# An order of weight sums and splits ahead of and in a squared-ReLU MLP

## The chip, the cores and the metric

The kernel is one program on one core of a Trainium2 chip. The metric is the device time of one execution in microseconds (us). TensorE (PE) multiplies, VectorE (DVE) and ScalarE (ACT) do elementwise work, GpSimd (POOL) and SyncE (SP) here mostly issue transfers (DMAs); each engine runs its instructions in the order in which they stand.

## The reference

One layer of an encoder over 512 tokens of width 1024: a token mixer of recurrent heads, cross-attention over 256 memory tokens, and an MLP of hidden width 4096, with a residual each and a final RMSNorm. All in float32:

```python
for l in range(DEPTH):                       # DEPTH = 1
    x = x + token_mixer(rmsnorm(x, norm_mix[l]), w_in[l], b_in[l], ...)
    x = x + cross_attention(rmsnorm(x, norm_xattn[l]), rmsnorm(mem, norm_mem[l]), w_xq[l], w_xkv[l], w_xo[l])
    x = x + squared_relu_mlp(rmsnorm(x, norm_mlp[l]), w_up[l], w_down[l])
return rmsnorm(x, norm_final)

def squared_relu_mlp(xn, w_up, w_down):
    return jnp.square(jax.nn.relu(xn @ w_up)) @ w_down
```

## The kernel before, in words

**Products.** Every float32 operand is split into a high part (a copy rounded to the type that TensorE takes, by ScalarE) and a low part (the rest, by VectorE), both at L348 in `split_out`. A product is then three matmuls: high by high, high by low, low by high. For weights the tiles are `st` (a block of 128 x 1024 as loaded), `wh` and `wl` (its high and low part); each has three buffers. In the MLP `xT` and `yT` hold the parts of the input of the up product, `a` those of the hidden activations.

**Seven products for eight.** The MLP is four up stages and four down stages in turn (`st` 0 to 7, even ones up). Each is a blocked product done with seven products P1 to P7 in place of eight, in two halves g (written a and b: "7b" is half 1 of P7). P1 to P3 take a block of the weights as it is, P4 to P7 sums of blocks, and the inputs are sums likewise ("forms": `form(p, g, ...)`, built and split by VectorE and ScalarE). The list `MJ` gives the order in which the 14 halves of each stage are multiplied; in the first up stage it is 1a 1b 2a 2b 5a 5b 6a 6b 7a 7b 4a 3a 4b 3b, so its entry n = 9 is 7b. In down stages it is P1, P5, P6, P2, P7, P3, P4, each as a, b (P1, P5, P2, P6, P3, P7, P4 in the last).

**Sums of weights.** For the up stages, and in part for the down stages, they are made ahead of the MLP in HBM (`form_<stage>_<product>_<half>`): SyncE writes a first block (`start`) or copies another sum (`follow`, L321, a P4 sum from the P6 sum), GpSimd adds a block by an accumulating transfer (`add`, L305). `make_forms` gives the order of these steps, and `allow(n)` lets some of them go at each weight block: a budget to which n is added, of which a step of SyncE takes 1 and an add 2. `weights()`, called for each block of the stream ahead of the MLP, calls `allow`; so does `mahead()` inside the later products. A step of GpSimd is made to wait (`after`) for the last low split that was made, a step of SyncE stands behind (`behind`, an order on its engine without a wait) the last load of weights. GpSimd's adds stand in one row with its other work: the powers of the norms (L214, L1081, L1448) and accumulating loads of sums for the attention's output product (L1187).
The rest of the down stages' sums are made in two buffers in SBUF (`msum`, in the profile `as`): `sum_base` loads the first block by SyncE, `sum_add` adds by GpSimd. `due` says at which weight block they are issued: for P5 of the next down stage at n + 3 and n + 7.

**Order on the engines.** PE's order is written by hand; ACT and DVE are put in order by a scheduler after what is ready, with `behind` and `tc.high_priority()` as its marks. `msplit` splits weight block n and loads it if `mload` hasn't; `mahead(n)` splits up to n + 2 and loads up to n + 6. SyncE issues weight loads from L269 (the stream) and from L305 and L1239 (`mload`: blocks as they are, and the sums in HBM).

**Other lines.** L1490 builds P7's input of the first up stage from two others, L1493 that of P3; L1623 and L1628 take products of the first up stage out of the accumulators; L1556 and L1557 are ReLU and square (`square`), L1565 to L1583 subtractions and additions for the forms of a down stage, L1527 adds a product of a down stage to the residual (`add_to`), L1518 is the last scaling of a row tile, and L1519 its store. The dictionary `turn` gives after which product a form is built.

## Time and profile before

| | |
|---|---|
| three runs | 828.56, 827.82, 826.29 us (median 827.82) |
| profiled execution | 825.79 us, of which the span of the instructions 824.0 us |
| mean granted clock of TensorE | 0.998 |
| PE busy | 803.1 us (97%) |
| DVE, ACT, POOL busy | 618.6, 486.1, 95.4 us |
| weight splits at L348 (`wh`, `wl`) | 165 each, 1058 and 1224 ns |
| transfers | 167.26 MB, mean 203 GB/s |
| GpSimd's adds for sums in HBM | 44, 512 KB each, 9.0 us from issue to landing (median) |
| SyncE's copies between sums | 18, 512 KB each, 10.2 us to landing |
| SyncE's weight loads `st<-in_wpk` | 123, 512 KB each, 4.4 us to landing |

Times in rows are us from the start of the span; a row of a timeline gives start, length, engine, line, operation, out<-in, and in brackets for how long the engine stood idle ahead of it and who released it. `...` in a row of rows stands for rows left out.

### The profile page before, as it was taken

The page shows a single profiled execution, that of the slowest core. Times are in us where ns is not written, and L with a number is a line of the kernel's source. Part 1 is how long each engine was busy: PE and PEld are TensorE (multiplying, and loading weights), DVE is VectorE, ACT ScalarE, POOL GpSimd, SP SyncE. Part 2 cuts the span into 40 slices and gives each one's busy share as a digit, 9 for nine tenths or more (in the row PEclk, how much of TensorE's full clock was granted, in tenths as well). Part 3 has the DMA queues.
Part 4 walks back from the last instruction along what each step waited for, and adds up shares of the span by engine and source line. Part 5 has one row for each costly group of instructions (what it writes and reads, how often), then busy time and mean ns, then how long its engine had stood idle before and what let it go on. Part 6 is the DMA issues. An engine that isn't in the chain of part 4 may idle for free.

```text
span 824.0 us, 14080 instructions
## 1 busy us (share of the span) xinstructions
PE 803.1 (97%) x5438; PEld 693.2 (84%) x5438; DVE 618.6 (75%) x1033; ACT 486.1 (59%) x854; POOL 95.4 (12%) x130
## 2 busy tenths in 40 slices
PE   8999999999999999999999999899999999999995
PEld 6788788886888989887888889887998899789984
DVE  6568975699469988555567979897489658875995
ACT  5247464445578475455545678773586458546854
POOL 2000111220230011221111003010001000100001
PEclk9999999999999999999999999999999999999999
DMA  7368889588688676887884357768866696668552
GB/s 278 118 238 257 216 181 280 174 197 254 159 230 252 198 221 203 237 193 218 203 224 108 85 122 212 248 163 247 267 199 158 218 282 198 180 200 266 179 153 103
DMA packets 56597, 167.26 MB, mean 203 GB/s; under 512 B 5393, under 2 KB 5521, under 8 KB 56530
## 3 DMA queue, kind: packets, MB, share of 16 engines
q1 hardware_dynamic: 41200, 126.04, 43.7%
q0 software_dynamic: 15040, 39.85, 26.8%
q8 instruction: 43, 0.70, 0.3%
q10 hardware_dynamic: 290, 0.47, 0.2%
q14 instruction: 24, 0.20, 0.1%
HBM read 164.24 MB, written 48.23 MB: 258 GB/s over the span
## 4 chain that ended last, share of the span: by engine, by line
PE 72%; DVE 11%; DMA 6%; issue 5%; ACT 5%; POOL 1%; POOLq 0%; ACTq 0%; DVEq 0%
PE mm L351 11%; PE mm L352 11%; PE mm L353 11%; PE sm L1315 5%; PE sm L1316 4%; PE sm L1314 4%; DVE wl L348 4%; PE sm L1604 2%; DMA st<-in_wpk 2%; PE sm L1605 2%; PE sm L1603 2%; ACT wh L348 2%; DMA st<-form_P 2%; PE mm L1604 1%; PE mm L1605 1%
## 5 line engine op out<-in xcount | busy, mean ns | idle before, releaser
L348 DVE TENSOR_TENSOR wl<-st,wh 128x1024 fp32r<-128x1024 f32 x165 | 201.5, 1224 | 104.0 <-ACT wh L348 103.1
L348 ACT ACTIVATE wh<-st 128x1024 fp32r<-128x1024 f32 x165 | 174.2, 1058 | 171.2 <-PE mm L352 44.0
L351 PE MATMUL mm<-xT,wh 128*128 128x512 f32 x288 | 115.5, 402 | 0.0
L353 PE MATMUL mm<-xT,wl 128*128 128x512 f32 x288 | 113.1, 393 | 0.1
L352 PE MATMUL mm<-xT,wh 128*128 128x512 f32 x288 | 112.8, 392 | 0.3 <-DVE xT L1066 0.3
L305 POOL DMA_DIRECT2D form_P<-in_wpk x44 | 44.7, 1059 | 289.1 <-DVE wl L348 243.5
L1315 PE MATMUL sm<-wl,a 128*128 128x512 f32 x180 | 70.4, 391 | 1.8 <-DVE wl L348 1.8
L1314 PE MATMUL sm<-wh,a 128*128 128x512 f32 x180 | 70.3, 391 | 0.1
L1316 PE MATMUL sm<-wh,a 128*128 128x512 f32 x180 | 70.1, 390 | 0.0
L353 PEld LDWEIGHTS mm<-xT,wl 128*128 128x128 f32 x288 | 54.1, 188 | 11.8 <-DVE wl L348 0.3
L352 PEld LDWEIGHTS mm<-xT,wh 128*128 128x128 f32 x288 | 54.2, 188 | 10.9 <-DVE xT L1066 0.9
L351 PEld LDWEIGHTS mm<-xT,wh 128*128 128x128 f32 x288 | 54.1, 188 | 10.9 <-ACT wh L348 0.3
L305 POOL DMA_DIRECT2D as<-in_wpk x20 | 17.6, 915 | 262.0 <-DVE wl L348 159.8
L1315 PEld LDWEIGHTS sm<-wl,a 128*128 128x128 f32 x180 | 33.8, 188 | 10.0 <-DVE wl L348 3.0
L1314 PEld LDWEIGHTS sm<-wh,a 128*128 128x128 f32 x180 | 33.8, 188 | 7.6 <-ACT wh L348 0.5
L1316 PEld LDWEIGHTS sm<-wh,a 128*128 128x128 f32 x180 | 33.8, 188 | 6.9
L1603 PE MATMUL sm<-yT,wh 128*128 128x256 f32 x128 | 36.3, 284 | 1.7 <-ACT yT L348 1.7
L1604 PE MATMUL sm<-yT,wh 128*128 128x256 f32 x128 | 36.3, 284 | 0.9 <-DVE yT L348 0.9
L1604 PE MATMUL sm<-xT,wh 128*128 128x256 f32 x128 | 36.4, 284 | 0.3 <-DVE xT L348 0.2
L1604 PE MATMUL mm<-xT,wh 128*128 128x256 f32 x128 | 36.3, 284 | 0.2 <-DVE xT L348 0.2
L1603 PE MATMUL sm<-xT,wh 128*128 128x256 f32 x128 | 36.4, 284 | 0.0
L1603 PE MATMUL mm<-xT,wh 128*128 128x256 f32 x128 | 36.3, 284 | 0.0
(388 smaller groups left out, 2114.6 us busy)
## 6 DMA issues: line engine op xcount, KB each, us to landing
st<-in_wpk SPq DMA_DIRECT2D x123, 512.0 KB, 4.4
form_P<-in_wpk POOLq DMA_DIRECT2D x44, 512.0 KB, 9.0
st<-form_P SPq DMA_DIRECT2D x42, 512.0 KB, 5.8
form_P<-in_wpk SPq DMA_DIRECT2D x26, 512.0 KB, 8.0
as<-in_wpk POOLq DMA_DIRECT2D x24, 512.0 KB, 8.4
form_P<-form_P SPq DMA_DIRECT2D x18, 512.0 KB, 10.2
gate<-in_wpk POOLq DMA_DIRECT2D x8, 512.0 KB, 5.8
as<-form_P SPq DMA_DIRECT2D x8, 512.0 KB, 6.6
```

Source lines behind the costliest of these rows:

```text
L305: return eng.dma_start(out=dst, in_=mblock(st, g, *b), max_dma_last_dim=4096, **kw)
L348: return sc.activation(dst_hi, src, AF.Copy), v.tensor_tensor(out=dst_lo, in0=src, in1=dst_hi.bitcast(F32), op=ALU.subtract)
L351: pe.matmul(ps, lhsT=ah, rhs=bh, start=first, stop=False)
L352: pe.matmul(ps, lhsT=ah, rhs=bl, start=False, stop=False)
L353: pe.matmul(ps, lhsT=al, rhs=bh, start=False, stop=last)
L1314: pe.matmul(ps, lhsT=ah, rhs=bh, start=new, stop=False, **fl)
L1315: pe.matmul(ps, lhsT=ah, rhs=bl, start=False, stop=False, **fl)
L1316: pe.matmul(ps, lhsT=al, rhs=bh, start=False, stop=end and k == 1, **fl)
L1603: pe.matmul(o, lhsT=hi[:, z], rhs=xh[:, m], start=new, stop=False, **fl)
L1604: pe.matmul(o, lhsT=hi[:, z], rhs=xl[:, m], start=False, stop=False, **fl)
L1605: pe.matmul(o, lhsT=lo[:, z], rhs=xh[:, m], start=False, stop=kt == 3, **fl)
```

## The change

It has five parts.

1. The budget of `allow` is 1.25 rather than 1 for the blocks of the keys and values, and stays at 2.5 (was 2) from block 45 on; `mahead` calls `allow` only for the MLP's own blocks. All steps of `make_forms` then stand ahead of the MLP.
2. In the first up stage the split of 7b's weights stands behind the split of P7's input (`early["P7"]`).
3. In the down stages the split of the weights of P5 half 1, rather than half 0, stands behind the P5 form of half 1. The sums of P5 for the next down stage are issued at n + 5 and n + 9, and their add waits for the last low split.
4. In `up`: the forms of P7 half 0 are built in a later turn; other turns are moved; the subtraction and square for P2 stand behind P5's.
5. In the last stage the final scaling of row tile t - 2 stands behind the add of tile t.

```diff
-        allow(0 if i < 6 else 1 if key[1] == "kv" else 2.5 if i < 45 else 2)
+        allow(0 if i < 6 else 1.25 if key[1] == "kv" else 2.5)
...
     def sum_add(st, p, g):
         o = mfill(gp, msum[p != "P5"][:, g * 1024:g * 1024 + 1024], st, g, (1, 0) if p == "P4" else (0, 0), True)
-        behind(o, last_made[0])
+        (after if p == "P5" else behind)(o, last_made[0])
...
-            if st % 2 and (p, g) == ("P5", 0):
-                for a, b in zip(made, early["P5", 1]):
+            if st % 2 and (p, g) == ("P5", 1) or n == 9:
+                for a, b in zip(made, early["P7" if n == 9 else ("P5", 1)]):
                     behind(a, b)
...
-                due.append((n + 3, sum_base, st + 2, q, g))
-                due.append((n + 7, sum_add, st + 2, q, g))
+                m = n + (5 if p == "P5" else 3)
+                due.append((m, sum_base, st + 2, q, g))
+                due.append((m + 4, sum_add, st + 2, q, g))
...
-        if n % 2:
+        if n % 2 and n >= len(JOBS):
             allow(2)
...
-        p7 = split_out(*xf["P7"], x1)
+        p7 = early["P7"] = split_out(*xf["P7"], x1)
...
         if not fin:
             return
+        if c == 1 and t > 1:
+            behind(ends[t - 2][0], added)
...
         def first(g):
-            v.tensor_tensor(out=y[3, g], in0=y[2, g], in1=y[3, g], op=ALU.subtract)
+            early["diff"] = v.tensor_tensor(out=y[3, g], in0=y[2, g], in1=y[3, g], op=ALU.subtract)
...
         def by_p5(g):
             z = y[1, g]
-            v.tensor_tensor(out=z, in0=C[g], in1=z, op=ALU.subtract)
-            square(z, z)
+            taken = v.tensor_tensor(out=z, in0=C[g], in1=z, op=ALU.subtract)
+            squared = square(z, z)
+            if st and g:
+                behind(taken, early["diff"])
+                behind(squared, early["P5", 1][0])
...
         def by_p3(g):
-            v.tensor_tensor(out=y[1, g], in0=y[1, g], in1=y[3, g], op=ALU.add)
+            o = v.tensor_tensor(out=y[1, g], in0=y[1, g], in1=y[3, g], op=ALU.add)
+            behind(o, early["diff"])
...
                     second(g)
-                    by_p7(g)
...
-        turn = ((("P1", 1), second, 1), (("P5", 1), by_p3, 0), (("P6", 0), by_p7, 1), (("P2", 0), by_p3, 1))
+        turn = ((("P1", 1), second, 1), (("P5", 1), by_p7, 0), (("P6", 0), by_p3, 0), (("P6", 1), by_p7, 1), (("P2", 1), by_p3, 1))
         if st == 6:
-            turn = ((("P1", 1), second, 1), (("P5", 1), by_p3, 0), (("P2", 0), by_p3, 1), (("P6", 0), by_p7, 1))
+            turn = ((("P1", 1), second, 1), (("P5", 1), by_p3, 0), (("P2", 0), by_p3, 1), (("P2", 1), by_p7, 0), (("P6", 0), by_p7, 1))
```

No instruction is added or removed, and PE's order is the same. What moves on the other engines is shown at three places; line numbers of the kernel after are some lines higher (L1623 is L1631 there).

GpSimd, from the scale of the cross-attention (L1081) to the last sum in HBM; L1448 is the norm ahead of the MLP. Before:

```order
L1081 TENSOR_TENSOR misc_75<-tiny_591_4073,misc_75 128x4
L305 DMA form_4_P6_0_2611<-in_wpk 256x1x512
L305 DMA form_6_P6_0_2623<-in_wpk 256x1x512
L305 DMA form_4_P6_1_2615<-in_wpk 256x1x512
L305 DMA form_6_P6_1_2627<-in_wpk 256x1x512
L1187 DMA as_660_4480<-in_wpk 128x1024 x4
L305 DMA form_4_P4_0_2612<-in_wpk 256x1x512
...
L1448 TENSOR_TENSOR tiny_773_5047<-tiny_772_5044,misc_75 128x2
L1448 TENSOR_TENSOR tiny_790_5132<-tiny_789_5129,misc_75 128x2
L305 DMA form_6_P4_0_2624<-in_wpk 256x1x512
L305 DMA form_4_P4_1_2616<-in_wpk 256x1x512
L305 DMA form_6_P4_1_2628<-in_wpk 256x1x512
```

The same stretch after, from the first P6 add (L1449 is L1448 of before, and stands behind these rows):

```order
L305 DMA form_4_P6_0_2611<-in_wpk 256x1x512
L305 DMA form_6_P6_0_2623<-in_wpk 256x1x512
L305 DMA form_4_P6_1_2615<-in_wpk 256x1x512
L305 DMA form_6_P6_1_2627<-in_wpk 256x1x512
L1081 TENSOR_TENSOR misc_75<-tiny_591_4078,misc_75 128x4
L305 DMA form_4_P4_0_2612<-in_wpk 256x1x512
L305 DMA form_6_P4_0_2624<-in_wpk 256x1x512
L305 DMA form_4_P4_1_2616<-in_wpk 256x1x512
L1187 DMA as_660_4486<-in_wpk 128x1024
L305 DMA form_6_P4_1_2628<-in_wpk 256x1x512
L1187 DMA as_660_4486<-in_wpk 128x1024 x3
```

The four P6 adds have moved ahead of L1081, and the three adds that stood behind L1448 have moved ahead of it, to the sums for the attention's output.

ScalarE in the first up stage, around the start of product 7a (`yT_698` is the high part of P7's input, `wh_827` of 7b's weights, `wh_834` and `yT_694` of 3a's, `wh_838` of 4b's weights). Before, then after:

```order
L348 ACTIVATE xT_693_4658<-a4_769_5035 128x1024
L348 ACTIVATE wh_827_5411<-st_811_5278 128x1024
L1623 ACTIVATE rg_700_4667<-sm_796_5142 128x512
L348 ACTIVATE yT_698_4665<-a4_751_4936 128x1024
L348 ACTIVATE wh_830_5442<-st_816_5316 128x1024
L1623 ACTIVATE rg_700_4667<-sm_802_5187 128x512
L348 ACTIVATE wh_834_5478<-st_821_5350 128x1024
L348 ACTIVATE yT_694_4661<-a4_782_5077 128x1024
```

```order
L348 ACTIVATE xT_693_4661<-a4_769_5038 128x1024
L1631 ACTIVATE rg_700_4670<-sm_796_5145 128x512
L348 ACTIVATE yT_698_4668<-a4_751_4939 128x1024
L348 ACTIVATE wh_827_5411<-st_811_5280 128x1024
L348 ACTIVATE wh_830_5442<-st_816_5317 128x1024
L1631 ACTIVATE rg_700_4670<-sm_802_5189 128x512
L348 ACTIVATE wh_834_5478<-st_821_5351 128x1024
...
L348 ACTIVATE wh_838_5514<-st_826_5384 128x1024
L348 ACTIVATE yT_694_4664<-a4_782_5080 128x1024
```

The split of 7b's weights has moved behind that of P7's input, and the split of 3a's input behind that of 4b's weights. VectorE's low parts move in the same way (`yT_699` ahead of `wl_828`, `wl_839` ahead of `yT_695`).

VectorE in down stage 1, ahead of the low part of P5's weights (`wl_859` before, `wl_858` after; `a4_852`, `a4_844` before are forms of the hidden activations, L1527 adds into the residual):

```order
L348 TENSOR_TENSOR gate_848_5592<-rg_700_4667,gate_848_5592 128x512
L1570 TENSOR_TENSOR rg_700_4667<-mm_822_5353,rg_700_4667 128x512
L348 TENSOR_TENSOR a4_852_5627<-t2_823_5378,a4_852_5627 128x512
L348 TENSOR_TENSOR a4_844_5556<-as_791_5134,a4_844_5556 128x512
L1575 TENSOR_TENSOR t2_823_5378<-t2_823_5378,as_792_5135 128x512
L1527 TENSOR_TENSOR vv_528_3650<-vv_528_3650,sm_856_5664 128x512
L348 TENSOR_TENSOR wl_859_5667<-st_840_5518,wh_858_5666 128x1024
```

```order
L348 TENSOR_TENSOR gate_847_5588<-rg_700_4670,gate_847_5588 128x512
L348 TENSOR_TENSOR wl_858_5663<-st_840_5518,wh_857_5662 128x1024
L348 TENSOR_TENSOR a4_851_5623<-t2_823_5378,a4_851_5623 128x512
L1574 TENSOR_TENSOR rg_700_4670<-mm_822_5353,rg_700_4670 128x512
L1582 TENSOR_TENSOR t2_823_5378<-t2_823_5378,as_792_5138 128x512
L1528 TENSOR_TENSOR vv_528_3652<-vv_528_3652,sm_855_5660 128x512
```

The low split has moved ahead of five half-size steps.

## The prediction

> **What bounds the kernel now.** I read the page first, for the engine that carries the span.

> ```profile
> PE 803.1 (97%) x5438; PEld 693.2 (84%) x5438; DVE 618.6 (75%) x1033; ACT 486.1 (59%) x854; POOL 95.4 (12%) x130
> PEclk9999999999999999999999999999999999999999
> q0 software_dynamic: 15040, 39.85, 26.8%
> ```

> TensorE is busy for 803.1 of 824.0 us at a full clock, and the change leaves its instructions and their order alone. So only the holes in the matmul stream, 824.0 - 803.1 = 20.9 us, can be won, and a loss must show as a new hole. [...]

> The waits of TensorE say which holes the change can touch:

> ```profile
> PE sm L1315 <- DVE wl L348: 1.8, 3, 0.7
> PE sm L1603 <- ACT yT L348: 1.7, 1, 1.7
> ```

> Columns: total us, times, longest. L1603 to L1605 are the products of the up stages, L1314 to L1316 those of the down stages. Next the timeline of TensorE at these places (start, length):

> ```profile
> 518.12 0.28 PE L1605 MATMUL sm<-yT,wl 128*128 128x256 f32 x1
> 520.15 0.38 PE L1603 MATMUL sm<-yT,wh 128*128 128x256 f32 x1 [1.75 <-ACT yT L348]
> 521.41 0.38 PE L1604 MATMUL sm<-yT,wh 128*128 128x256 f32 x1 [0.88 <-DVE yT L348]
> 521.63 0.28 PE L1605 MATMUL sm<-yT,wl 128*128 128x256 f32 x1
> ...
> 527.02 0.28 PE L1605 MATMUL sm<-yT,wl 128*128 128x256 f32 x1
> 527.14 0.28 PE L1603 MATMUL sm<-xT,wh 128*128 128x256 f32 x1
> ...
> 544.13 0.39 PE L1314 MATMUL sm<-wh,a 128*128 128x512 f32 x1
> 545.19 0.50 PE L1315 MATMUL sm<-wl,a 128*128 128x512 f32 x1 [0.67 <-DVE wl L348]
> ...
> 566.86 0.39 PE L1314 MATMUL sm<-wh,a 128*128 128x512 f32 x1
> 567.89 0.50 PE L1315 MATMUL sm<-wl,a 128*128 128x512 f32 x1 [0.64 <-DVE wl L348]
> ...
> 702.93 0.39 PE L1314 MATMUL sm<-wh,a 128*128 128x512 f32 x1
> 703.76 0.50 PE L1315 MATMUL sm<-wl,a 128*128 128x512 f32 x1 [0.44 <-DVE wl L348]
> ...
> 808.89 0.39 PE L1315 MATMUL sm<-wl,a 128*128 128x512 f32 x1
> 809.12 0.39 PE L1316 MATMUL sm<-wh,a 128*128 128x512 f32 x1
> 809.65 0.47 PE L1314 MATMUL sm<-wh,a 128*128 128x512 f32 x1
> ```

> Undisturbed starts are 0.12 us apart for 256 columns (527.02 to 527.14) and 0.23 for 512 (808.89 to 809.12). The holes are what goes beyond:
> - first up stage, start of product 7a: (520.15 - 518.12 - 0.12) + (521.41 - 520.15 - 0.12) = 1.91 + 1.14, and 0.22 - 0.12 = 0.10 behind it: 3.15 us;
> - P5 of down stage 1: 1.06 - 0.23 = 0.83; a later product's weights there (566.86): 1.03 - 0.23 = 0.80; P5 of down stage 5: 0.83 - 0.23 = 0.60; in the last stage 0.53 - 0.23 = 0.30. I add to each the 0.10 that was seen behind the first one, an estimate: 2.53 + 0.40 = 2.93 us.

> Together 6.1 us. That is all that this change can aim at.

> **Part 1, weight sums before the MLP.** Why 7a waits is in the timelines of ScalarE, VectorE and SyncE:

> ```profile
> 514.01 1.05 ACT L348 ACTIVATE xT<-a 128x1024 fp32r<-128x1024 f32 x1
> 517.61 1.06 ACT L348 ACTIVATE wh<-st 128x1024 fp32r<-128x1024 f32 x1 [2.56 <-DMA st<-form_P]
> 519.05 1.05 ACT L348 ACTIVATE yT<-a 128x1024 fp32r<-128x1024 f32 x1
> ...
> 514.80 1.22 DVE L1490 SCALAR_TENSOR_TENSOR a<-a,a 128x1024 f32<-128x1024 f32 x1
> 520.13 1.23 DVE L348 TENSOR_TENSOR yT<-a,yT 128x1024 fp32r<-128x1024 f32 x1 [0.20 <-ACT yT L348]
> ...
> 510.17 3.19 SPq L1239 DMA_DIRECT2D st<-form_P  x2
> ```

> The input of 7a exists at 514.80 + 1.22 = 516.02. But ScalarE's next instruction is the split of 7b's weights, whose load left at 510.17 and released it at 517.6, some 7.4 us later. The split of 7a's input stands behind it and starts at 519.05, three us after it could. The load shares the transfers with three sums:

> ```profile
> form_P<-in_wpk POOLq DMA_DIRECT2D x3, 512.0 KB, 9.9
> ...
> 380.00:400.00 20.00, 19.74 (x102) 16.21 (x100) 11.69 (x30) 10.29 (x28) 3.16 (x3) 1.00 0.63 167
> 400.00:420.00 20.00, 20.00 (x108) 16.98 (x107) 12.08 (x26) 11.61 (x26) 3.21 (x4) 1.00 0.81 210
> 500.00:520.00 20.00, 18.16 (x150) 17.76 (x148) 16.72 (x20) 14.57 (x20) 5.01 (x4) 1.00 0.93 257
> ```

> First row: the accumulating transfers that GpSimd issues between 500 and 525 (512 KB each, 9.9 us to land). Other rows: stretches; the last two columns are the DMA share and GB/s. The three adds move from this 0.93 stretch to before the MLP. Their price in transfer time: queue q0 takes 26.8% of 824.0 us for about 39.85 MB / 0.524 MB = 76 transfers, so 2.9 us of all engines each, 8.7 us for three. From 380 to 420, where the adds ahead of them now stand, there are free 20 x (0.37 + 0.19) = 11.2 us. They fit, with 2.5 us left; I cost them at nothing there, and what covers them is the lead of the weight loads, which are a transfer ahead of their splits. If that lead is gone, rival A or B holds. GpSimd also issues sums ahead of its own small powers, and SyncE meets the copies of the last four sums (each waiting for the landing of another sum) a few weight loads earlier; both are priced with the rivals. The budget's other raise (1 to 1.25) shifts earlier sums by a load or two; same cover, nothing.

> **Part 2, order around 7a.** Independently of the load, 7b's split now stands behind the split of 7a's input on both engines. ScalarE can start that input at 516.02 and ends at 516.02 + 1.05 = 517.07, VectorE at 517.07 + 1.23 = 518.30; the second matmul would start at 518.12 + 0.12 + 0.12 = 518.36 and sees the result a little after 518.30. I leave 0.25 us, between nothing and 0.5 (a hand-over of 0.2, as in the 0.20 of the row at 520.13, and one more). So of 3.15 us 2.9 go. What is late next: 7b's weights, ScalarE 517.07 + 1.06 = 518.13, VectorE 518.30 + 1.22 = 519.5, used after 7a, near 521.2; covered.

> **Part 3, what that exposes.** By the order the split of 3a's input now stands behind the high split of 4b's weights, on VectorE behind the low one. That buffer comes free when 7b ends. Before, 7b ends and 4a starts at 527.14; 2.9 us earlier this is 524.24. Then 1.06 + 1.04 on ScalarE, to 526.34, but VectorE: 524.24 + 1.06 + 1.22 + 1.23 = 527.75. 4a is 24 matmuls of 0.12 = 2.9 us, so 3a starts at 527.14 and its second matmul at 527.26: a new hole of 0.5, with hand-overs (0.2) 0.75. Bounds 0 (the engines swap nothing that is late) and 1.2.

> **Part 4, P5 and its neighbours in the down stages.**

> ```profile
> 541.38 2.00 ACT L348 ACTIVATE wh<-st 128x1024 fp32r<-128x1024 f32 x2
> ...
> 543.91 1.22 DVE L348 TENSOR_TENSOR wl<-st,wh 128x1024 fp32r<-128x1024 f32 x1
> ...
> 565.52 1.06 ACT L348 ACTIVATE wh<-st 128x1024 fp32r<-128x1024 f32 x1 [3.61 <-DMA st<-in_wpk]
> ```

> In down stage 1 VectorE's low split starts at 543.91, while the high one that it needs is the first of the two from 541.38, ready at 542.4. In the new order it stands five half-size steps further ahead (by the order; some 0.6 us each), so it follows at once: 542.4 + 1.22 = 543.6, before the matmul at 544.13 + 0.23 = 544.36. The hole of 0.93 goes, with 0.7 us to spare. At 565.52 ScalarE waited 3.61 us for a load that shares the transfers with sums of the next P5 form; their transfers now start two weight loads later, which frees more than the 0.90 that are missing. In stage 5 the steps of the other half leave VectorE's queue ahead of the low split in the same way; 0.70 goes too. If the sums merely collide two loads later, 0.9 comes back: bounds 0 and 0.9 of loss; I take 0, since the stage's other loads show no hole behind them. The added wait of the P5 add on the newest low split keeps GpSimd from nothing but the next sums, which are used a stage later. The steps that now stand behind the split (P7 and P2 forms) have at least one more product, 24 x 0.23 = 5.5 us, ahead of their use.

> **Part 5, the last stage.**

> ```profile
> 807.49 1.42 DVE L1518 SCALAR_TENSOR_TENSOR vv<-vv,tiny,rg 128x512 f32<-128x512 f32 x2 [0.57 <-POOL tiny L1545]
> 808.82 0.68 DVE L1527 TENSOR_TENSOR vv<-vv,sm 128x512 f32<-128x512 f32 x1
> ```

> The add that frees TensorE's bank waits behind two final scalings of 1.42 us. Behind the add these cost nothing: only their stores follow. 0.40 goes.

> **Sum.** 6.1 gone, 0.25 stay and 0.75 are new: 6.1 - 1.0 = 5.1 us. The profiled execution took 825.79 us (span 824.0), 2.0 below the median of the runs, 827.82. It would be 820.7; carried to the median 822.7. The smallest difference that a measurement of this kernel can tell is about 0.3%, 2.5 us.

> **Rivals.**
> *A, the loads before the MLP starve, slower.* The accumulates now stand among weight loads, and SyncE issues the sums' copies in order with those loads:

> ```profile
> SPq L321 <- DMA form_P<-in_wpk: 15.5, 4, 8.8
> ...
> 380.69 1.06 ACT L348 ACTIVATE wh<-st 128x1024 fp32r<-128x1024 f32 x1
> 387.98 1.06 ACT L348 ACTIVATE wh<-st 128x1024 fp32r<-128x1024 f32 x1 [1.02 <-PE mm L352]
> ```

> A copy that waits for an accumulate held SyncE up to 8.8 us; a load beside them takes as long as the sums' 9.9; 18.7 us together. Splits are 7.3 us apart (380.69 to 387.98), so with a load two splits ahead about 14.6 are covered: 4.1 us for one such meeting. It decides from two meetings on: 8.2 - 5.1 = 3.1 us slower, 830.9. For it: the stretches at 380 to 420 would fill to over 0.9, as 500 to 520 was. Against it: the waits of TensorE name no weight load there now, and 2.5 us of transfer time stay free. [...] Chance 0.08.
> *B, one such meeting.* 5.1 - 4.1 = 1.0 us won, 826.8, no change that can be told. Chance 0.12.
> *C, GpSimd's powers come late.* Between the two powers of the attention heads an add now stands:

> ```profile
> 293.85 1.01 POOL L214 TENSOR_TENSOR tiny<-tiny,misc 128x4 f32<-128x4 f32 x1 [3.20 <-DVE tiny L212]
> 294.89 0.69 DVE L684 TENSOR_TENSOR t<-t,tiny 128x512 f32<-128x512 f32 x1 [0.80 <-POOL tiny L214]
> ```

> GpSimd was idle for 3.20 us there, and an issue is 1.05; but it waits for a split to finish first. VectorE waits for the power already, so each us late is a us lost. There are three such places by the order (between this pair of powers, two adds ahead of the next pair, and four ahead of L1081); at 0.8 us each, the wait that VectorE shows now doubled: 2.4 lost, 5.1 - 2.4 = 2.7 won, 825.1. Chance 0.12.
> *D, the change doesn't do what it says.* The load of 7b is still late for other reasons, and the new places give back the down stages' share: 2 to 2.5 us of gain, 825.6. Against it: part 2 needs no faster load. Chance 0.06.

> **How the numbers follow.** The forecast has 0.62: 822.7, its own range from 820.7 (the 1.0 us of parts 2 and 3 at nothing, and one more us won where loads come sooner) to 824.5 (1.2 in place of 0.75 at 3a, 0.9 given back in the down stages, 0.5 in place of 0.25 at 7a). C and D lie at the bound of 2.5 us, so each is halved. Faster by over 0.3%: 0.62 + 0.06 + 0.03 = 0.71. Same: 0.11 (B) + 0.06 + 0.03 = 0.20. Slower: 0.08 (A) + 0.01 (B, where one meeting is worse than priced) = 0.09. The range goes from 820.5 to 826.8, B's time; A and the tails stay outside.

> **What would show it.** Right: TensorE starts 7a within 0.5 us of 6b's end; no accumulate issued by GpSimd between 500 and 515; a hole of 0.5 to 1 us at 3a, released by VectorE; no hole over 0.3 us at P5 of stages 1 and 5; no matmul waiting between 360 and 440. Wrong: holes at L351 to L353 released by the weight splits, with ScalarE waiting for a load (A, B); the span up to 500 us longer through L691 (C); ScalarE still held by a load ahead of yT (D).

## The result and the profile after

| | before | after |
|---|---|---|
| median | 826.38 us (6 runs, 825.39 to 828.56) | 820.75 us (6 runs, 820.55 to 821.30) |
| profiled execution | 825.79 us, span 824.0 | 820.77 us, span 818.9 |
| mean granted clock | 0.998 (profiled execution) | 0.996 to 0.998 |

The ratio of the times is 0.9928, 95% interval 0.9915 to 0.9942: faster by 0.72%. The medians differ by 5.6 us, the two profiled executions by 5.0, their spans by 5.1.

The page of the kernel after, busy time:

```profile
PE 802.7 (98%) x5438; PEld 693.6 (85%) x5438; DVE 618.1 (75%) x1033; ACT 487.0 (59%) x854; POOL 95.1 (12%) x130
```

TensorE's work is unchanged (802.7 against 803.1 us), and the holes sum to 818.9 - 802.7 = 16.2 us in place of 20.9. The waits of TensorE, the one row that is new against before:

```profile
PE mm L1612 <- DVE yT L348: 0.5, 1, 0.5
```

The two rows shown of before (L1315 and L1603) are gone. The timeline of TensorE at the same matmuls (7a, 3a, P5 of down stage 1, last stage; lines are 8 higher in the up stages, 1 in the down stages):

```profile
518.63 0.28 PE L1611 MATMUL sm<-yT,wh 128*128 128x256 f32 x1
518.81 0.39 PE L1612 MATMUL sm<-yT,wh 128*128 128x256 f32 x1
...
527.42 0.28 PE L1611 MATMUL mm<-yT,wh 128*128 128x256 f32 x1
528.17 0.39 PE L1612 MATMUL mm<-yT,wh 128*128 128x256 f32 x1 [0.47 <-DVE yT L348]
528.39 0.28 PE L1613 MATMUL mm<-yT,wl 128*128 128x256 f32 x1
...
542.25 0.39 PE L1315 MATMUL sm<-wh,a 128*128 128x512 f32 x1
542.48 0.39 PE L1316 MATMUL sm<-wl,a 128*128 128x512 f32 x1
...
804.49 0.39 PE L1317 MATMUL sm<-wh,a 128*128 128x512 f32 x1
804.71 0.39 PE L1315 MATMUL sm<-wh,a 128*128 128x512 f32 x1
```

At 7a 0.06 us is left (0.18 - 0.12), at 3a there is a new hole of 0.63 + 0.10 = 0.73, and the down stages run at 0.23 without a gap. Both kernels have the same 5438 matmuls in one order, so their starts can be compared one by one: the kernel after is 0.38 us behind when 7a should start, wins 2.98 there, loses 0.73 at 3a and wins 3.19 behind it, 5.06 in all. The rows behind this, ScalarE and VectorE around 7a:

```profile
516.44 1.05 ACT L348 ACTIVATE yT<-a 128x1024 fp32r<-128x1024 f32 x1
517.40 1.04 ACT L348 ACTIVATE wh<-st 128x1024 fp32r<-128x1024 f32 x1
...
517.53 1.23 DVE L348 TENSOR_TENSOR yT<-a,yT 128x1024 fp32r<-128x1024 f32 x1 [1.13 <-ACT yT L348]
...
526.89 1.22 DVE L348 TENSOR_TENSOR yT<-a,yT 128x1024 fp32r<-128x1024 f32 x1
```

ScalarE splits 7a's input at 516.44 (519.05 before) and 7b's weights behind it, without a wait. The load of 7b's weights, issued at 510.17 before and at 510.55 after, with the us from issue to landing in the last column, before and then after:

```profile
st<-form_P SPq DMA_DIRECT2D x1, 512.0 KB, 7.4
...
st<-form_P SPq DMA_DIRECT2D x1, 512.0 KB, 3.3
```

And by stretches (length; busy us of TensorE, its weight loads, VectorE, ScalarE and GpSimd; granted clock; DMA share; GB/s):

```profile
380.00:400.00 20.00, 19.74 (x102) 16.27 (x101) 11.77 (x31) 10.27 (x26) 3.13 (x3) 1.00 0.93 249
400.00:420.00 20.00, 20.00 (x109) 16.95 (x107) 12.00 (x28) 11.63 (x26) 2.67 (x3) 1.00 0.60 136
...
500.00:520.00 20.00, 19.77 (x164) 19.46 (x164) 18.35 (x22) 15.96 (x23) 2.27 (x1) 1.00 0.65 231
```

The DMA share of 500 to 520 fell from 0.93 to 0.65, that of 380 to 400 rose from 0.63 to 0.93, and TensorE is as busy there as before.

### The profile page after: what moved, and what is told of

Its sections match the earlier page's. It is cut to its first block, busy times and chain, and to the rows that moved or that the text cites. A ratio compares the mean times of both kernels' runs of the same rounds, so it can differ in the third digit from the quotient of the medians.

```text
span 818.9 us, 14080 instructions
## 1 busy us (share of the span) xinstructions
PE 802.7 (98%) x5438; PEld 693.6 (85%) x5438; DVE 618.1 (75%) x1033; ACT 487.0 (59%) x854; POOL 95.1 (12%) x130
## 3 DMA queue, kind: packets, MB, share of 16 engines
q0 software_dynamic: 15040, 39.85, 27.2%
## 4 chain that ended last, share of the span: by engine, by line
PE 87%; DVE 6%; issue 2%; ACT 2%; POOL 1%; DMA 1%; POOLq 0%; ACTq 0%; DVEq 0%
PE mm L351 12%; PE mm L352 12%; PE mm L353 12%; PE sm L1317 6%; PE sm L1316 6%; PE sm L1315 6%; PE sm L1612 4%; PE sm L1613 3%; PE sm L1611 3%; PE mm L1612 3%; PE mm L1613 3%; PE mm L1611 3%; DVE wl L348 2%; PE mm L1316 2%; PE mm L1317 2%
## 5 line engine op out<-in xcount | busy, mean ns | idle before, releaser
L348 DVE TENSOR_TENSOR wl<-st,wh 128x1024 fp32r<-128x1024 f32 x165 | 201.5, 1223 | 94.5 <-ACT wh L348 93.6
L348 ACT ACTIVATE wh<-st 128x1024 fp32r<-128x1024 f32 x165 | 174.2, 1058 | 159.5 <-PE mm L352 44.0
L351 PE MATMUL mm<-xT,wh 128*128 128x512 f32 x288 | 115.5, 402 | 0.0
L353 PE MATMUL mm<-xT,wl 128*128 128x512 f32 x288 | 113.1, 393 | 0.1
L352 PE MATMUL mm<-xT,wh 128*128 128x512 f32 x288 | 112.8, 392 | 0.3 <-DVE xT L1066 0.3
L1315 PE MATMUL sm<-wh,a 128*128 128x512 f32 x180 | 70.1, 389 | 0.0
L1316 PE MATMUL sm<-wl,a 128*128 128x512 f32 x180 | 70.0, 389 | 0.0
L353 PEld LDWEIGHTS mm<-xT,wl 128*128 128x128 f32 x288 | 54.1, 188 | 11.7 <-DVE wl L348 0.3
L352 PEld LDWEIGHTS mm<-xT,wh 128*128 128x128 f32 x288 | 54.2, 188 | 11.0 <-DVE xT L1066 0.9
L351 PEld LDWEIGHTS mm<-xT,wh 128*128 128x128 f32 x288 | 54.1, 188 | 10.8 <-ACT wh L348 0.3
L1316 PEld LDWEIGHTS sm<-wl,a 128*128 128x128 f32 x180 | 33.8, 188 | 7.0
L1315 PEld LDWEIGHTS sm<-wh,a 128*128 128x128 f32 x180 | 33.8, 188 | 7.0
L348 ACT ACTIVATE wh<-as 128x1024 fp32r<-128x1024 f32 x24 | 25.4, 1058 | 22.6 <-PE sm L1317 14.2
L1612 PE MATMUL sm<-yT,wh 128*128 128x256 f32 x128 | 36.3, 284 | 0.0
## 6 DMA issues: line engine op xcount, KB each, us to landing
st<-in_wpk SPq DMA_DIRECT2D x123, 512.0 KB, 4.4
form_P<-in_wpk POOLq DMA_DIRECT2D x44, 512.0 KB, 8.8
st<-form_P SPq DMA_DIRECT2D x42, 512.0 KB, 4.4
form_P<-in_wpk SPq DMA_DIRECT2D x26, 512.0 KB, 8.6
as<-in_wpk POOLq DMA_DIRECT2D x24, 512.0 KB, 8.1
form_P<-form_P SPq DMA_DIRECT2D x18, 512.0 KB, 9.9
gate<-in_wpk POOLq DMA_DIRECT2D x8, 512.0 KB, 6.0
as<-form_P SPq DMA_DIRECT2D x8, 512.0 KB, 4.8
```

Of the source, the lines that this page charges most:

```text
L348: return sc.activation(dst_hi, src, AF.Copy), v.tensor_tensor(out=dst_lo, in0=src, in1=dst_hi.bitcast(F32), op=ALU.subtract)
L351: pe.matmul(ps, lhsT=ah, rhs=bh, start=first, stop=False)
L352: pe.matmul(ps, lhsT=ah, rhs=bl, start=False, stop=False)
L353: pe.matmul(ps, lhsT=al, rhs=bh, start=False, stop=last)
L1315: pe.matmul(ps, lhsT=ah, rhs=bh, start=new, stop=False, **fl)
L1316: pe.matmul(ps, lhsT=ah, rhs=bl, start=False, stop=False, **fl)
```

## The experiments

Spans in this section are those of the profiled execution.

**One part alone: the sums.** The kernel before with the first edit only:

```diff
-        allow(0 if i < 6 else 1 if key[1] == "kv" else 2.5 if i < 45 else 2)
+        allow(0 if i < 6 else 1.25 if key[1] == "kv" else 2.5)
...
-        if n % 2:
+        if n % 2 and n >= len(JOBS):
             allow(2)
```

> The kernel before with part 1 alone (all sums in HBM ahead of the MLP; the order of splits as before). Theory, the queue: 7b's load, no longer beside GpSimd's sums, takes 3.3 us like those that go alone, so ScalarE doesn't wait for it, but 7b's split still stands ahead of 7a's input: ScalarE 515.06 + 1.06 + 0.58 + 1.05 = 517.75, VectorE to 519.0, a hole of about 0.6 us at 7a in place of 3.15. The four holes of the down stages (2.9 us in all) stay. Span 824.0 - 2.5 = 821.5 us. Rival, the transfers: the sums were all there was to the late load, the hole goes to under 0.2, span 820.9; and by the rival of starving loads a new hole of 1 us or more at L351 to L353 between 360 and 440, span 822.5 or more.

Measured: 824.70 us, ratio 0.9969 (0.9958 to 0.9981), span 822.7. TensorE, ScalarE and VectorE at 7a:

```profile
518.45 0.28 PE L1603 MATMUL sm<-yT,wh 128*128 128x256 f32 x1
519.45 0.39 PE L1604 MATMUL sm<-yT,wh 128*128 128x256 f32 x1 [0.72 <-DVE yT L348]
...
515.64 1.06 ACT L348 ACTIVATE wh<-st 128x1024 fp32r<-128x1024 f32 x1 [0.39 <-PE sm L1604]
517.09 1.05 ACT L348 ACTIVATE yT<-a 128x1024 fp32r<-128x1024 f32 x1
...
518.17 1.23 DVE L348 TENSOR_TENSOR yT<-a,yT 128x1024 fp32r<-128x1024 f32 x1 [0.20 <-ACT yT L348]
```

The load of 7b's weights lands 3.3 us after its issue, as in the kernel after, and no longer holds ScalarE. The order that is left costs 0.88 + 0.10 us, somewhat over the 0.6 of the queue's theory and far from nothing. No new hole came up between 360 and 440. The gain at 7a is 2.2 us out of 3.15: the down stages' holes stay, and one of 0.47 appeared at 780, so the span lies 1.2 over the expected 821.5.

**One part alone: the order at 7a.** The kernel before with 7b's split behind that of P7's input:

```diff
-            if st % 2 and (p, g) == ("P5", 0):
-                for a, b in zip(made, early["P5", 1]):
+            if st % 2 and (p, g) == ("P5", 0) or n == 9:
+                for a, b in zip(made, early["P7" if n == 9 else ("P5", 1)]):
...
-        p7 = split_out(*xf["P7"], x1)
+        p7 = early["P7"] = split_out(*xf["P7"], x1)
```

> The kernel before with part 2 alone (7b's split behind that of P7's input in the first up stage; the sums stay where they were, three of them in the MLP's first stage). Theory, the queue: the late load is harmless once nothing that 7a needs stands behind it: hole at 7a 0.1 to 0.3 us, 7b's own weights ready by 519.8, before they are used; a hole of 0.5 to 0.9 at 3a only if 4b's split stands ahead of 3a's input here too. The other holes stay. Span 821.0 to 822.0 us. Rival, the transfers: the loads behind the sums come late all the same, and ScalarE waits for them further on, the hole only moves to 7b or 4a: gain under 1 us, span over 823.

Measured: 828.13 us, ratio 1.0018 (1.0003 to 1.0033), span 824.7. My theory fell, the rival held: the hole moved. TensorE at the start of 3a, and ScalarE ahead of it:

```profile
526.67 0.28 PE L1605 MATMUL sm<-xT,wl 128*128 128x256 f32 x1
528.74 0.38 PE L1603 MATMUL mm<-yT,wh 128*128 128x256 f32 x1 [1.79 <-ACT yT L348]
530.26 0.38 PE L1604 MATMUL mm<-yT,wh 128*128 128x256 f32 x1 [1.14 <-DVE yT L348]
...
523.89 1.06 ACT L348 ACTIVATE wh<-st 128x1024 fp32r<-128x1024 f32 x1 [3.70 <-DMA st<-in_wpk]
526.70 1.04 ACT L348 ACTIVATE wh<-st 128x1024 fp32r<-128x1024 f32 x1
527.65 1.04 ACT L348 ACTIVATE yT<-a 128x1024 fp32r<-128x1024 f32 x1
```

No hole is left at 7a, but ScalarE now waits 3.70 us for the next load beside the sums (3a's weights), and 3a's input stands behind that: 1.95 + 1.40 us. Behind this hole the granted clock was 0.50 for 3.4 us, from 530.6 on, which cost 1.5 us more. Would the order help if it were mended at 3a as well?

```diff
-            if st % 2 and (p, g) == ("P5", 0):
-                for a, b in zip(made, early["P5", 1]):
+            if st % 2 and (p, g) == ("P5", 0) or n in (9, 12):
+                for a, b in zip(made, early[{9: "P7", 12: "P3"}.get(n, ("P5", 1))]):
...
-        p7 = split_out(*xf["P7"], x1)
+        p7 = early["P7"] = split_out(*xf["P7"], x1)
...
-        split_out(*xf["P3"], x3_)
+        early["P3"] = split_out(*xf["P3"], x3_)
```

Entry 12 is 4b: its split now stands behind that of 3a's input.

> The kernel before with only the order of splits in the first up stage: 7b's behind P7's input, 4b's behind 3a's input; the sums stay, three of them in that stage. Theory, loads and queue together: in the kernel with 7b's split alone moved, ScalarE and VectorE waited for the load of 3a's own weights (9.1 us beside the sums), and everything behind it was late; VectorE's low split and L1493 stand behind that load here too, ready at about 527.4, then 1.04 + 1.23 for the two parts of 3a's input: a hole of 2 to 3 us at 3a, span 823.5 to 824.5. Rival, order alone: the hole at 3a came from 4b's split only, it goes to under 0.8 us, span under 822.

Measured: one run, 830.89 us, span 829.1; a hole of 2.29 + 1.14 + 0.26 at 3a. The load of 3a's weights took 9.7 us, ScalarE waited 3.93 us for it, and L1493, which builds 3a's input, stands on VectorE behind the low split of these weights. So in this first stage order alone doesn't do; as long as the sums are there, it is the load that is late. This kernel also has new holes in later stages (1.77 at 813, 0.95 at 705, 0.75 at 785), where the scheduler's order came out otherwise. And behind the hole at 3a the granted clock (third from the end) was at half, in all from 529.5 to 536.4:

```profile
530.80:533.00 2.20, 2.20 (x12) 2.20 (x12) 2.20 (x3) 2.20 (x5) 0.00 (x0) 0.50 0.20 45
533.00:536.00 3.00, 3.00 (x16) 3.00 (x16) 1.72 (x4) 1.05 (x3) 0.00 (x0) 0.50 0.80 251
```

That is 2.6 us lost besides the hole, and the next experiment sets out to size it.

**A hole of set size.** In the kernel after, ScalarE writes the high part of 7a's input k times more ahead of its split:

```diff
+        for _ in range(k):
+            sc.activation(xf["P7"][0], x1, AF.Copy)
         p7 = early["P7"] = split_out(*xf["P7"], x1)
```

> The kernel after with the high part of 7a's input written twice more by ScalarE (same values) ahead of its split: a hole of set size, some 2 x 0.96 = 1.9 us, at 7a and nothing late behind it. Theory, the clock: a hole of this size leaves the granted clock at 1.00 and costs its length: 820.75 + 1.9 = 822.7 us, runs as close together as those of the kernel after (0.75 us). Rival, length alone: the same.

> The same with three more writes: a hole of about 2.9 us, near the 3.15 of the kernel before. Theory, the clock: near the size at which the two kernels with holes of 3.4 us at 3a fell to a granted clock of 0.50 for 2.8 and 5.4 us; in some executions it falls and costs 1.4 to 2.7 us more, so the runs spread over 2 us or more, between 823.6 and 826.4, as those of the kernel before do. Rival, length alone: 823.6 us, spread under 1 us.

> The same with five more writes: a hole of about 4.8 us. Theory, the clock: it falls to 0.50 in nearly every execution for 2.8 to 5.5 us and costs 1.4 to 2.7 us on top of the length: 820.75 + 4.8 + 2.1 = 827.6 us, between 826.9 and 828.3. Rival, length alone: 825.5 us.

Measured: 824.16 us (k = 2, 822.69 to 825.73), 825.94 (k = 3, 823.81 to 827.08) and 827.44 (k = 5, 826.70 to 828.86). Stretches of the three, in this order, cut at the recorded changes of the clock, in pieces of 3.41 us (the clock is third from the end):

```profile
519.59:523.00 3.41, 1.59 (x11) 1.19 (x10) 1.98 (x2) 3.38 (x5) 0.00 (x0) 1.00 0.21 81
523.00:526.41 3.41, 3.41 (x19) 3.41 (x18) 2.66 (x3) 0.37 (x1) 0.00 (x0) 0.50 0.52 156
```

```profile
516.94:520.35 3.41, 1.54 (x13) 1.34 (x12) 0.00 (x0) 3.35 (x5) 0.00 (x0) 1.00 0.49 184
520.35:523.77 3.42, 2.24 (x8) 1.95 (x9) 2.94 (x3) 2.34 (x3) 0.00 (x0) 0.50 0.02 5
523.77:527.18 3.41, 3.41 (x17) 3.41 (x17) 1.70 (x2) 0.00 (x0) 0.00 (x0) 0.50 0.62 195
```

```profile
519.38:522.79 3.41, 0.00 (x0) 0.00 (x0) 0.00 (x0) 3.35 (x5) 0.00 (x0) 1.00 0.01 2
522.79:526.20 3.41, 2.30 (x9) 2.01 (x10) 3.00 (x3) 2.28 (x3) 0.00 (x0) 0.50 0.03 5
526.20:529.61 3.41, 3.41 (x18) 3.41 (x18) 2.77 (x3) 0.03 (x1) 0.00 (x0) 0.50 0.68 197
```

Behind each hole TensorE runs at half clock, and its matmuls start 0.22 us apart (523.63 to 523.85) instead of 0.12 (k = 2):

```profile
523.63 0.41 PE L1613 MATMUL sm<-yT,wh 128*128 128x256 f32 x1
523.85 0.41 PE L1614 MATMUL sm<-yT,wh 128*128 128x256 f32 x1
```

Compared matmul by matmul with the kernel after, the three lost 2.18, 3.61 and 5.78 us in the hole itself, more than the 1.9, 2.9 and 4.8 expected, and 1.49, 2.23 and 2.25 us more in the half-clock stretch behind it. These three executions were each the slowest of their ten. In the medians, length alone would give 822.9, 824.4 and 826.5 us, and what was measured lies 1.2, 1.6 and 0.9 above. So a hole of this kind does cost more than its length, also for k = 2, where the theory expected none of it. For k = 3 and 5 the times fell near or in the ranges of the clock's theory, for k = 5 in part because a longer hole made up for a smaller price of the clock. The two stretches at 0.50 that the expectation for k = 3 puts at 2.8 and 5.4 us lasted 3.4 and 6.9 us. Among the ten executions with k = 3 the one with a mean clock of 0.997 took 823.81 us, those with 0.992 and 0.993 took 826.6 to 827.1: the same hole costs 3 us or 6.

What the traces show of the difference is how busy TensorE was ahead of the half clock. The half-clock stretches of the three are 3.41 us long (k = 2) and twice that (k = 3 and 5). In the trace of before the recorded clock is 1.00 from 4.29 to 820.07 us, in that of the kernel after from 5.67 to 814.63: 815.78 and 808.96 us, which are 239 and 237 pieces of 3.413 us. The half clock begins at 523.00, 520.35 and 522.79 us in the three, not whole pieces apart, so the edges lay elsewhere in each execution. Counted on from 4.29 us in such pieces, an estimate from these lengths, an edge at 519.70 cut the hole of 3.05 us at 7a in the profiled execution of before:

```profile
516.29:519.70 3.41, 2.12 (x18) 1.91 (x16) 0.99 (x1) 2.09 (x3) 0.00 (x0) 1.00 1.04 342
519.70:523.11 3.41, 2.08 (x15) 1.89 (x16) 3.21 (x4) 1.83 (x3) 0.00 (x0) 1.00 1.07 301
```

TensorE was busy for 0.62 and 0.61 of the two pieces, and the clock stayed at 1.00. In the piece ahead of the half clock it was busy for 1.59 of 3.41 us (0.47) with k = 2, for 1.54 (0.45) with k = 3 and not at all with k = 5. In the traces of before and after every piece up to the last matmul held 0.56 or more (the least is 1.91 us, 4.29 to 7.70 of before) and had the full clock behind it; the first one without a matmul (816.66 to 820.07 of before, 811.22 to 814.63 of after) had the half clock behind it.

**The sums still earlier, for the price of the starving of loads.**

```diff
-        allow(0 if i < 6 else 1.25 if key[1] == "kv" else 2.5)
+        allow(0 if i < 6 else 4)
```

> The kernel after with a budget of 4 per weight block from the start (in place of 1.25 and 2.5), so that the last sum in HBM stands ahead of the small powers near 290 us. It prices the starving of loads: the last 20 adds or so then run between 200 and 290, where the DMA share was already 0.69 to 0.83, 2.9 us of all transfer engines each. Theory: the transfers fill, weight loads come late, holes at L351 to L353 released by weight splits of 4 to 10 us in all: time 824 to 831. Rival: the lead of the loads covers it as it did between 360 and 420, time as the kernel after within 1 us.

Measured: 847.82 us, ratio 1.025 (1.0209 to 1.0292). A stretch, ScalarE's waits between 140 and 330, and one of its rows:

```profile
140.00:160.00 20.00, 12.44 (x74) 11.26 (x73) 5.68 (x14) 5.45 (x22) 2.96 (x3) 0.83 1.03 280
...
ACT wh L348 <- DMA st<-in_wpk: 28.6, 6, 10.2
...
150.12 1.06 ACT L348 ACTIVATE wh<-st 128x1024 fp32r<-128x1024 f32 x1 [10.18 <-DMA st<-in_wpk]
```

The theory was right in kind and far too low in size (27 us slower than the kernel after, 3 to 10 expected): from 100 to 220 the DMA share was 1.03 to 1.09 in every 20 us, ScalarE waited up to 10.2 us for a load, and what TensorE then missed was not only weights but all that stood behind the split on ScalarE and VectorE (`as` at L638: 7.6 us, at L895: 6.2). The load behind the last row left at 137.6 and took 12.4 us, and SyncE stood 50.4 us at copies of sums between 100 and 330 (18.6 in the kernel after between 100 and 400), so slow transfers and late issues both have a part that this run doesn't tell apart. The clock was at 0.50 for 17 us in all between 151 and 301, which is a part of the loss too. In the kernel after the share is over 1.0 only for one such stretch (1.06 at 360 to 380, 1.03 before) and 0.93 in the next, and ScalarE waits for no load there.

**The down stages, part by part.** The P5 sums two blocks later, alone, and the order of P5's split, alone, both on the kernel before:

```diff
-        behind(o, last_made[0])
+        (after if p == "P5" else behind)(o, last_made[0])
...
-                due.append((n + 3, sum_base, st + 2, q, g))
-                due.append((n + 7, sum_add, st + 2, q, g))
+                m = n + (5 if p == "P5" else 3)
+                due.append((m, sum_base, st + 2, q, g))
+                due.append((m + 4, sum_add, st + 2, q, g))
```

> The kernel before with only the P5 sums of the next down stage issued two weight blocks later, their add with the wait. Theory: the hole of 0.9 at 566.9 came from the load beside these sums; it goes, the holes at 518 to 521 (3.15), 544 (0.93), 703 (0.70) and 809 (0.4) stay: span 823.1. Rival: the late load has another cause, or the sums collide two loads later, and the hole stays or moves within stage 1: span 823.8 to 824.3.

```diff
-            if st % 2 and (p, g) == ("P5", 0):
+            if st % 2 and (p, g) == ("P5", 1):
```

> The kernel before with only the order of the down stages' splits: the weights of P5 half 1, no longer half 0, behind the P5 form of half 1. Theory: P5's low split moves ahead on VectorE, the holes at 544 (0.93) and 703 (0.70) go, those at 518 to 521, 567 and 809 stay: span 822.4. Rival: the other order in the forms is needed as well (subtraction and square for P2 behind P5's), and one of the two holes stays: span 823.0 to 824.0.

Measured, one run each: spans 824.1 and 825.9. With the late sums the hole at 565 is gone, as expected, but P5's at 543 grew from 0.83 to 1.68, and one of 1.00 came up at 781:

```profile
543.41 0.39 PE L1315 MATMUL sm<-wh,a 128*128 128x512 f32 x1
545.32 0.50 PE L1316 MATMUL sm<-wl,a 128*128 128x512 f32 x1 [1.52 <-DVE wl L348]
...
544.05 1.22 DVE L348 TENSOR_TENSOR wl<-st,wh 128x1024 fp32r<-128x1024 f32 x1
```

VectorE makes this low split when it did before (544.05, before 543.91), and by lines and tiles the order on ScalarE and VectorE is that of before. TensorE comes 0.72 us sooner (543.41, before 544.13), 0.5 of it because its hole at 7a was shorter in this execution, and waits the longer for a split that is no earlier. At 781 it is the same. So the span is that of the rival.

With P5's order alone the holes at 544 and 703 are gone, but one of 0.49 comes at 705, and others at 722 (0.45 + 1.03), 786 (0.49) and in the last stage, where 0.30 became 1.11:

```profile
810.25 0.39 PE L1316 MATMUL sm<-wh,a 128*128 128x512 f32 x1
811.59 0.47 PE L1314 MATMUL sm<-wh,a 128*128 128x512 f32 x1 [0.95 <-DVE vv L1527]
```

Each edit takes away the hole that it is aimed at, and neither shows a net gain in its one run (824.1 and 825.9 against 824.0). In the second the order of ScalarE and VectorE does change behind the edit; in the first it is TensorE's own lead that is lost at the next late split. The moved forms in `up` have no run of their own. From the other side, two parts undone in the kernel after. The P5 sums issued as before:

```diff
-        (after if p == "P5" else behind)(o, last_made[0])
+        behind(o, last_made[0])
...
-                m = n + (5 if p == "P5" else 3)
-                due.append((m, sum_base, st + 2, q, g))
-                due.append((m + 4, sum_add, st + 2, q, g))
+                due.append((n + 3, sum_base, st + 2, q, g))
+                due.append((n + 7, sum_add, st + 2, q, g))
```

> The kernel after with the P5 sums of the next down stage issued as before (n + 3 and n + 7, without the wait). Theory: their transfers are again beside the load that ScalarE waited for near 565, and the hole of about 0.9 us there is back: span 819.8. Rival: the other changes already freed that load, no hole: span 818.9.

Measured: one run, span 821.3, 2.4 over the kernel after. No hole at 565, but holes of 0.74 and 1.03 at 640 and 720, in down stages 3 and 5, where ScalarE waits for loads:

```profile
638.12 1.06 ACT L348 ACTIVATE wh<-st 128x1024 fp32r<-128x1024 f32 x1 [4.49 <-DMA st<-form_P]
...
718.00 1.06 ACT L348 ACTIVATE wh<-st 128x1024 fp32r<-128x1024 f32 x1 [4.86 <-DMA st<-form_P]
```

Neither expectation named the place, but the mechanism of the theory, a load beside these sums, is what the rows show: the load behind the first one took 9.4 us, beside an add of GpSimd issued 0.9 us ahead of it, and 5.3 us in the kernel after. And the last stage without its edit:

```diff
-        if c == 1 and t > 1:
-            behind(ends[t - 2][0], added)
```

> The kernel after without part 5 (the final scaling of row tile t - 2 no longer behind the add of tile t). Theory: in the last stage the add that frees TensorE's bank waits behind two scalings again, a hole of 0.3 to 0.4 us near 804, span 819.3. Rival: with the MLP's other holes gone the scalings fall elsewhere, no hole, span 818.9.

Measured: span 819.2; TensorE's add waits behind two scalings again:

```profile
804.29 0.39 PE L1317 MATMUL sm<-wh,a 128*128 128x512 f32 x1
804.83 0.47 PE L1315 MATMUL sm<-wh,a 128*128 128x512 f32 x1
```

A hole of 0.54 - 0.23 = 0.31 us, as the theory had it.

**The hole at 3a mended.** The kernel after, with 4b's split (n = 12) behind the split of 3a's input:

```diff
-            if st % 2 and (p, g) == ("P5", 1) or n == 9:
-                for a, b in zip(made, early["P7" if n == 9 else ("P5", 1)]):
+            if st % 2 and (p, g) == ("P5", 1) or n in (9, 12):
+                for a, b in zip(made, early[{9: "P7", 12: "P3"}.get(n, ("P5", 1))]):
...
-        split_out(*xf["P3"], x3_)
+        early["P3"] = split_out(*xf["P3"], x3_)
```

> The kernel after, and in the first up stage the split of 4b's weights also stands behind the split of 3a's input, on ScalarE and VectorE. Theory: the hole at 3a (0.75 us in the kernel after) came from that order alone and goes; 4b's weights, used one product of 2.9 us later, are still in time. Span 818.9 - 0.7 = 818.2 us, time about 820.0. Rival: the scheduler's order behind it changes as well, and 4b or a product of the first down stage gets a hole of the same size: span 818.7 to 819.5, no gain.

Measured: 820.03 us (six runs), ratio to before 0.9921 (0.9905 to 0.9938), span 818.0. TensorE at 3a:

```profile
527.01 0.28 PE L1611 MATMUL mm<-yT,wh 128*128 128x256 f32 x1
527.25 0.39 PE L1612 MATMUL mm<-yT,wh 128*128 128x256 f32 x1
```

Of 0.63 us 0.12 is left (0.24 - 0.12), and no other hole came up in the MLP. The span is 0.9 shorter, the median 0.7; but 0.4 of the span was won ahead of the MLP (the first of the two rows stands at 527.42 in the kernel after), where the edit changes nothing, and 0.5 at 3a. The intervals of the two ratios overlap, so that it is the faster kernel rests on the hole that went, not on the times.

## Why the prediction was right or wrong

- **What bounds, and the 6.1 us of holes.** Right. All five holes went, in the places named.
- **Part 1, sums.** Right in what they do: the load of 7b's weights lands 3.3 us after its issue instead of 7.4, with the sums alone too, and no matmul waits for a weight load between 360 and 440. The place was wrong. Of the 8.7 us of transfer time that were to fill 380 to 420, 20 x (0.30 - 0.21) = 1.8 stand there. Between 260 and 360 the shares of the five stretches rose by 0.47 in sum (from 0.60 to 0.84 each, to 0.67 to 0.96), so 9.4 us more stand there.
- **Part 2, order at 7a.** The hole went (0.06 left, 0.25 said). But "independently of the load" and rival D's "part 2 needs no faster load" were wrong: with the order alone the wait moves to the next load, and the time does not fall. The sums alone take 2.2 of the 3.15 us; the order is worth the other 0.8 only once the load is in time.
- **Part 3, the new hole at 3a.** Right, 0.73 against 0.75, and its cause is shown by the kernel that mends it.
- **Part 4, down stages.** Right in the sum: with part 5, 2.93 us were said, and 3.19 are won behind 3a. That a step alone shows no gain, the sum did not say.
- **Part 5.** Right: 0.40 said, 0.31 measured without it.
- **Rivals.** A and B did not happen; A's mechanism is real, and the kernel with the larger budget shows it at a higher price. C: GpSimd's second power started straight behind an add, and VectorE's wait at L684 grew from 0.80 to 0.91, not by 0.8.
- **The sum and its carrying over.** Within the profiled executions 5.1 us were said, and 5.0 (5.1 in the spans) came: 820.7 forecast, 820.77 measured. That it fits so closely is in part luck: 5.4 us were won in the MLP, and 0.38 lost ahead of it, 0.10 of that at L691, where rival C looked for it. The step that failed is the next one, "carried to the median 822.7". It took the 2.0 us by which the median of before lay over its profiled execution as a constant that stays, and gave no reason for that. It doesn't stay: the median after is that of the profiled execution (0.02 below), and the time is 1.95 us under the forecast, at the low end of its own range. Nor is it a fixed number of before: it is 0.6 us for the six runs, and 53 later executions of before, in sets of 25, 21 and 7, have medians from 826.59 to 828.09, 0.8 to 2.3 above.

What the runs show in its place is a price of the hole at 7a that not every execution pays. Before's 3.05 us hole is of the size that with k = 3 cost 3 us in one execution and up to 6 in others, and the profiled execution of before, with a mean clock of 0.998, kept 1.00 on both sides of the edge at 519.70. Of these 53 executions of before, 27 have a mean clock under 0.996; of the 22 of kernels without a large hole in this stage (the sums alone, the kernel after, and the three variants of it that leave 7a as it is and add no hole) none has. In the set of 25, those under 0.996 have a median of 828.56 us, the others of 826.52. An estimate from the shares above: lay pieces of 3.413 us over the matmuls of before's trace with their edges at every place, and let the half clock follow on a share up to a limit between 0.47 (followed by it with k = 2) and 0.55 (0.56 was not followed by it in before); then it comes at 7a in 0.6 to 0.9 of the places. In the kernel after it comes in none, since any 3.41 us between 500 and 545 hold at least 0.86 there; with the sums alone the 0.98 us at 7a leave 0.71. So the term was not a constant but about 2 us in some half of before's executions, and it goes with the hole. Two things stay open: none of the traces is of an execution of before with the half-clock stretch, and the clock isn't the whole spread, since the eight executions of the sums alone run from 822.96 to 825.20 us at 0.996 to 0.998.

## What to carry to other kernels

When a transfer is late, an order that moves one step from behind it only passes the wait to the next step on that queue, here to 3a with 1.95 + 1.40 us; free the transfer and mend the order together, and test each alone before adding their gains. A hole in TensorE's stream like those here (2.18 to 5.78 us) should be priced with a possible half-clock stretch behind it, 1.49 to 2.25 us more here, and one profiled execution doesn't show how often that comes; the mean clocks of many runs do (27 of 53 under 0.996). And a hole that goes brings TensorE sooner to the next late split (at 543 us it came 0.72 us sooner, and the hole grew from 0.83 to 1.68), so single edits can each show no gain though together they give all of it.
